# A forgetting-attention trunk on one core: the first projections taken chunk by chunk with the stream, in an order written by hand

## The chip, the core and the metric

The kernel runs on one core of a Trainium2 chip. The metric is the device time of one execution in microseconds. The engines are named as in the profile: PE (TensorE), PEld (its weight loads), DVE (VectorE), ACT (ScalarE), POOL (GpSimd) and SP (SyncE, which here only starts transfers). A *bank* below is a tile of 128 partitions by 512 float32 numbers into which PE adds up products.

## What is computed

Two layers on a stream of 512 tokens by 1024 features, float32. The first layer is forgetting attention (FoX), the second latent attention; each has an MLP with squared ReLU behind it. The change concerns the beginning of the first layer:

```python
h = rms_norm(x, norm_mix_g[0])
proj = h @ w_in                          # columns: q 1024, k 1024, v 1024, gate 16
cum = cumsum(log_sigmoid(f_logit + b_f)) # 16 heads, along the 512 tokens
s = q @ k.T / 8 + cum[query] - cum[key]  # 16 heads of 64, causal
ctx = softmax(s) @ v
x = x + ctx @ w_out
```

## The kernel before, in words

**Products.** Every float32 operand of a product is split into a high part (a cast on ACT to the format that PE multiplies fastest) and a low part (the difference, on DVE). A product is then three matmuls (`three`, L260): high by high, high by low, low by high. A matmul here is mostly 128x128 weights by 512 columns.

**Weights.** They come in pieces of up to 128x1024 (`PIECES`, L74). `fetch` (L205) starts the transfer of a piece on SP's queue into one of two buffers `raw`. `cast_piece` (L210) makes the high part `whi` on ACT, `low_piece` (L223) the low part `wlo` on DVE; each has three buffers. `piece` (L250) hands out the next piece, after it has emitted this and the one behind it.

**The stream.** It lies turned, features on partitions, in eight chunks of 128x512 (`xs[0]` to `xs[7]`). `scaled` (L282) multiplies a chunk by the norm's gain and splits it into `h[k]`. The norm's factor rstd, one number for each token, is not needed for these products and is put in when a bank is emptied.

**FoX's beginning (L471 to L559).** It is written product by product, each over all eight chunks: the gate (16 columns in a block of 128 whose rest is zero, 24 matmuls into the bank `fps`), the queries of the first two heads (24), the sums of squares over the features as matmuls with a column of ones (`token_sums`, L297) and their reciprocal root (`rsqrt_mean`, the Newton steps on POOL), the keys of the first two heads (24), rstd spread to a 128x512 tile (`rstd_tile`, L341: four matmuls and a copy), and the values of eight heads (four pieces of 24 matmuls, 96 in all, into four banks, two of the tag `sc` and two of the tag `tp`, one for each block of 128 tokens). After the first value piece the queries and keys are emptied (`qk_parts`, L494) and the forget gate is worked out (`forget_sums`, L522): a log-sigmoid on 16 partitions, then running sums along the 512 tokens in nine doubling steps of a copy and an addition each on DVE. The result goes to DRAM (`csc`) and comes back broadcast over 128 partitions (`nb`, in `start`, L576), two heads at a time. The value banks are emptied in eight halves (`value_parts`, L512).

**What sets the order.** The engines run their instructions in one fixed order each, which a scheduler works out when the program is built. Where the list `order["on"]` names an engine, its instructions are tied to the order in which they are written (L113 to L122). At FoX's beginning it names none before the change.

**The attention (L408).** The steps are one block of 128 queries of a pair of heads each, 32 in all: scores on PE, then `soft_step` (L379) on DVE and ACT, then, three steps later, the transposes of the weights on PE and the product with the values. So that PE has work while the softmax runs, `Filler` (L347) deals out other products: the queries and keys of the next pairs (`proj`), the other eight heads' values, and the beginning of the output projection. `FILL1 = (12, 18)` are the matmuls dealt out at each step and at the end of each pair. `fill.run(12)` (L643) deals out twelve ahead of the first scores.

Nearly all instructions are issued by the helper on L112 (L113 after the change), so that the profile tells them apart by their tiles and not by their lines.

Of the kernel before, what the change touches and what calls it, by code (L numbers as in the profile page):

```python
# [11 lines left out]
F32 = mybir.dt.float32  # L12
# [23 lines left out]
RP1 = 40  # L36
RP2 = 14
RSQRT_BITS = 0x5F3759DF
MASK = -1.0e30
HALF = 512  # L40
CHUNKS = 3
# [32 lines left out]
def pieces():  # L74

    out = [("f", 128)]
    out += [("qk", 1024)] * 2 + [("v", 1024)] * 4
    for p in range(1, FH // 2):
        out += [("v4", 1024)] * (2 * V4_BEFORE.count(p)) + [("qk", 1024)] * 2
    out += [("fo", 1024)] * 8  # L80
    out += [("ffn0", 1024)] * 40
    out += [("ka", 1024)] * 6
    q = [("qb_r", 384), ("qb_n", 768)]
    out += [q[0], ("kvb_n", 1024), q[1], ("kvb_v", 1024)] + q + [("kvb_n", 1024)] + q + [("kvb_v", 1024)] + q
    out += [("mo", 1024)] * 8
    out += [("ffn1", 1024)] * 32
    return out
# [10 lines left out]
def trunk(ctx: ExitStack, tc: tile.TileContext, xT, wts, gains, fing, rope, out):  # L98
# [72 lines left out]


    gsb = const.tile([P, NG], F32, name="gsb")
    nc.scalar.dma_start(gsb, gains)
# [5 lines left out]
    nc.scalar.copy(warm, ones)  # L180

    maskz = const.tile([P, S], F32, name="maskz")
    nc.gpsimd.memset(maskz, 0.0)
# [24 lines left out]
        nc.sync.dma_start(raw[:, :w], wts[OFFS[n] : OFFS[n] + P * w].rearrange("(p w) -> p w", p=P))  # L208

    def cast_piece(n):  # L210
        name, w = PIECES[n]
# [3 lines left out]
        if name == "f":  # L215
            hi = hi.rearrange("p (k c) -> p k c", c=P)[:, :, :FH]
            nc.vector.memset(f32(state["ready"][n][0]), 0.0)
            nc.vector.memset(f32(lo), 0.0)
            nc.scalar.copy(hi, fetched[n][:, :w].rearrange("p (k c) -> p k c", c=FH))
        else:  # L220
            nc.scalar.copy(hi[:, :w], fetched[n][:, :w])

    def low_piece(n):  # L223
        name, w = PIECES[n]
        hi, lo = state["ready"][n]
        src, hi, lo = fetched.pop(n)[:, :w], hi[:, :w], lo[:, :w]
        if name == "f":
            src = src.rearrange("p (k c) -> p k c", c=FH)
            hi, lo = (t.rearrange("p (k c) -> p k c", c=P)[:, :, :FH] for t in state["ready"][n])
        nc.vector.tensor_tensor(lo, src, f32(hi), op=ALU.subtract)  # L230

    def beside_piece(n):

# [2 lines left out]
    def emit_piece(n):  # L236
        if n not in fetched:
            fetch(n)
        if n in APART:

            raw = fetched.pop(n)
            his, los = [rt(), rt()], [rt(), rt()]
            for j in range(2):
                split(raw[:, j * S : (j + 1) * S], his[j], los[j])
            state["ready"][n] = [(his[k // 4][:, c], los[k // 4][:, c]) for k in range(KD) for c in [slice(k % 4 * P, k % 4 * P + P)]]
            return
        cast_piece(n)
        low_piece(n)
# [56 lines left out]
    def rstd_of(acc, dim, mult=1.0, tag="tp"):  # L305

        return rsqrt_mean(token_sums(acc, tag), dim, mult)
# [155 lines left out]

    ctxs = []
    with ExitStack() as fx:
        vpool = fx.enter_context(tc.tile_pool(name="fox_v", bufs=12))
# [3 lines left out]
        xs = [tt() for _ in range(KD)]  # L470
        for k in range(KD):  # L471
            nc.sync.dma_start(xs[k], xT[:, k, :])
            if k == 0:
                emit_piece(0)
            if k == 3:
                emit_piece(1)
# [8 lines left out]
        qk = {}  # L485
        qk_ps = []
# [22 lines left out]

        v2 = {}  # L510

        def value_parts(q, tb, src):  # L512

            vt = vpool.tile([P, 4, 2, FHD], F32R, tag="v", name=nm("v"))
# [5 lines left out]
            v2[q, tb] = vt  # L520

        def forget_sums():  # L522

            z, e = tt(), tt()
            z, e = z[:FH], e[:FH]
            nc.vector.tensor_tensor(z, fps[:FH], rstd[:FH], op=ALU.mult)
            nc.vector.tensor_scalar_add(z, z, gsb[:FH, GCOL["bf"][0] : GCOL["bf"][0] + 1])
# [5 lines left out]
            nc.vector.scalar_tensor_tensor(out=cur, in0=z, scalar=0.0, in1=e, op0=ALU.min, op1=ALU.subtract)  # L533
            nc.vector.tensor_scalar_mul(cur, cur, -1.0)
# [8 lines left out]
            return csc  # L543

        accs = [bank(t) for t in ("sc", "sc", "tp", "tp")]
        for kp in range(4):
            whi, wlo = piece("v")
            for tb in range(NB):
                for k2 in range(2):
                    k = kp * 2 + k2  # L550
                    c = slice(k2 * S, (k2 + 1) * S)
                    t = slice(tb * P, (tb + 1) * P)
                    three(accs[tb], whi[:, c], wlo[:, c], h[k][0][:, t], h[k][1][:, t], k == 0, k == KD - 1, flip=True)
            if kp == 0:
                qk[0] = [qk_parts(pp, scale) for pp, scale in zip(qk_ps, QK_SCALES)]
                csc = forget_sums()
        for tb in range(NB):
            for q in range(2):
                value_parts(q, tb, accs[tb][:, q * 256 : (q + 1) * 256])  # L559

        def v4_gen(q):
            ws = [piece("v4"), piece("v4")]
            for tb in range(NB):
                pp = bank("acc")[:, :256]
                t = slice(tb * P, (tb + 1) * P)
                for k in range(KD):
                    whi, wlo = ws[k // 4]
                    c = slice(k % 4 * 256, k % 4 * 256 + 256)
                    three(pp, whi[:, c], wlo[:, c], h[k][0][:, t], h[k][1][:, t], k == 0, k == KD - 1, flip=True)
                    if k == 3:  # L570
                        yield 6
                value_parts(q, tb, pp)
                yield 6

        nbs = {}
# [791 lines left out]
def _pack(i):  # L1367
# [1 line left out]
    parts = []  # L1369
    fw = i["fox_w_in"][0]  # L1370
    parts.append(_cols(fw, 3 * W, FH))
    parts += [_cols(fw, 0, P), _cols(fw, W, P)]
    b = _cols(fw, 2 * W, S)
    parts += [b[:, 2 * kp : 2 * kp + 2] for kp in range(4)]
    for p in range(1, 8):
# [85 lines left out]
```

## Time and profile before

| | |
|---|---|
| median of 3 runs | 1138.52 us (1138.40 to 1138.56) |
| the profiled execution | 1139.54 us, of which the span from its first to its last instruction is 1137.7 us |
| granted TensorE clock, mean | 0.995 |
| PE busy | 1117.8 us, 98% of the span |
| DVE busy | 781.3 us, 69% |
| ACT busy | 582.0 us, 51% |

Times in the profile count from the start of the span. A row of the timeline reads: start, length, engine, line, operation, output and inputs with their shapes, count, and in brackets how long the engine had been idle and what released it. A row of the chain of waits reads: start, length, engine, tile, count; it follows the work that ended last back through what released it. A row of the table by stretch has the stretch's length, then busy time and number of instructions for PE, PEld, DVE, ACT and POOL, then the granted clock, the share of the DMA engines in use and GB/s. A row of the grouped lines has the group's shape and count, busy time and mean nanoseconds of one, and the idle time before them.

Up to 52.18 us, where the first scores stand, PE was busy for 47.15 us. From there to 231 us, where the attention ends, it was busy for 177.22 us of 178.82.

### The profile page before, as it was taken

What the parts mean: (1) busy time and instruction counts of PE and PEld (TensorE: products, weight loads), DVE (VectorE), ACT (ScalarE), POOL (GpSimd) and SP (SyncE); (2) the same over time, 40 slices, a digit from 0 to 9 for tenths busy, and PEclk for the clock granted to TensorE, in tenths of its full rate; (3) what the DMA queues carried; (4) which work ended last, traced back from release to release, by engine and by line L of the source; (5) the groups of instructions that cost most, each with busy time, mean ns of one, the idle gap of its engine ahead of it and who ended that gap; (6) DMA issues with size and microseconds to landing.
All of it is one profiled execution on the core that took longest, in us unless ns stands there. A gap on an engine that the chain in (4) does not pass through costs nothing.

```text
span 1137.7 us, 14266 instructions
## 1 busy us (share of the span) xinstructions
PE 1117.8 (98%) x5340; PEld 912.9 (80%) x5340; DVE 781.3 (69%) x1420; ACT 582.0 (51%) x1060; POOL 19.5 (2%) x71
## 2 busy tenths in 40 slices
PE   8999999999999999999999999999999999999996
PEld 5777887788888888888888777788888888888885
DVE  6797888864557676577795777737265775765785
ACT  5565655644555454444364566635465545444612
POOL 1000000001000000000001100000100000000000
PEclk9999999999999999999999999999999999999998
DMA  5422222143825315212344211313442511611402
GB/s 188 131 90 96 75 74 77 54 149 93 290 80 161 99 40 186 90 57 65 102 143 137 60 46 52 111 56 97 164 166 74 184 57 56 203 56 38 130 1 75
DMA packets 36822, 116.66 MB, mean 103 GB/s; under 512 B 4224, under 2 KB 4864, under 8 KB 36752
## 3 DMA queue, kind: packets, MB, share of 16 engines
q1 hardware_dynamic: 35888, 114.15, 31.0%
q10 hardware_dynamic: 864, 1.60, 0.4%
q8 instruction: 42, 0.69, 0.3%
q14 instruction: 28, 0.23, 0.1%
HBM read 109.40 MB, written 6.32 MB: 102 GB/s over the span
## 4 chain that ended last, share of the span: by engine, by line
PE 90%; DVE 5%; ACT 2%; DMA 1%; issue 1%; SPq 0%; ACTq 0%; DVEq 0%
PE up L112 34%; PE acc L112 18%; PE go L112 17%; PE sc L112 7%; PE tp L112 7%; PE keep L112 6%; ACT t L112 2%; DVE r L112 2%; DVE t L112 2%; DVE fs L112 1%; DMA raw<-wts 1%; DVE wlo L112 1%; ACT whi L112 0%; DMA nb<-csc 0%; DVE ptl L112 0%
## 5 line engine op out<-in xcount | busy, mean ns | idle before, releaser
L112 PE MATMUL acc<-r,whi 128*128 128x512 f32 x610 | 198.7, 406 | 4.9 <-ACT whi L112 4.9
L112 PE MATMUL up<-r,r 128*128 128x512 f32 x808 | 192.7, 391 | 0.0
L112 PEld LDWEIGHTS up<-r,r 128*128 128x128 f32 x808 | 151.3, 188 | 31.4
L112 PE MATMUL up<-r,whi 128*128 128x512 f32 x544 | 171.0, 391 | 0.0
L112 DVE TENSOR_TENSOR wlo<-raw,whi 128x1024 fp32r<-128x1024 f32 (+3 forms) x95 | 111.4, 1173 | 48.7 <-ACT whi L112 47.9
L112 DVE TENSOR_TENSOR t<-s,t 128x512 fp32r<-128x512 f32 x84 | 57.9, 690 | 122.1 <-ACT t L112 122.0
L112 PEld LDWEIGHTS acc<-r,whi 128*128 128x128 f32 x610 | 112.5, 191 | 30.9 <-ACT whi L112 5.3
L112 ACT CAST whi<-raw 128x1024 fp32r<-128x1024 f32 (+3 forms) x95 | 95.4, 1008 | 71.5 <-PE acc L112 33.0
L112 ACT ACTIVATE s<-up 128x512 f32<-128x512 f32 x56 | 33.4, 597 | 190.6 <-PE up L112 190.6
L112 PE MATMUL acc<-r,wlo 128*128 128x512 f32 x305 | 121.3, 398 | 0.1
L112 PEld LDWEIGHTS up<-r,whi 128*128 128x128 f32 x544 | 101.8, 188 | 20.8
L112 PE MATMUL up<-r,wlo 128*128 128x512 f32 x288 | 112.3, 390 | 0.0
L112 PE MATMUL go<-r,t 128*128 128x512 f32 x360 | 86.5, 390 | 0.0
L112 PE MATMUL sc<-r,r 128*128 128x512 f32 (+7 forms) x480 | 82.0, 358 | 2.2 <-ACT r L112 1.0
L112 PE MATMUL go<-whi,t 128*128 128x512 f32 x240 | 78.8, 390 | 0.0
L112 PEld LDWEIGHTS go<-r,t 128*128 128x128 f32 x360 | 67.6, 188 | 14.0
L112 PEld LDWEIGHTS sc<-r,r 64*128 64x128 f32 (+1 forms) x480 | 56.1, 186 | 26.7 <-issue 9.2
L112 PEld LDWEIGHTS acc<-r,wlo 128*128 128x128 f32 x305 | 58.3, 191 | 13.2 <-DVE wlo L112 0.4
L112 PEld LDWEIGHTS up<-r,wlo 128*128 128x128 f32 x288 | 54.1, 188 | 11.3
L112 DVE TENSOR_TENSOR r<-raw,r 128x512 fp32r<-128x512 f32 x72 | 46.5, 685 | 22.2 <-ACT r L112 22.2
L112 ACT ACTIVATE s<-s 128x512 f32<-128x512 f32 x64 | 40.5, 632 | 39.6 <-DVE s L112 37.8
L112 DVE TENSOR_TENSOR r<-q,r 128x512 fp32r<-128x512 f32 x94 | 60.5, 686 | 0.0
(199 smaller groups left out, 1862.5 us busy)
## 6 DMA issues: line engine op xcount, KB each, us to landing
raw<-wts SPq DMA_DIRECT2D x122, 512.0 KB, 3.5
q<-wts SPq DMA_DIRECT2D x56, 512.0 KB, 4.6
nb<-csc SPq DMA_DIRECT2D x8, 512.0 KB, 4.7
t<-xT SPq DMA_DIRECT2D x8, 256.0 KB, 6.2
r<-xT SPq DMA_DIRECT2D x8, 256.0 KB, 5.8
xmid<-r SPq DMA_DIRECT2D x8, 256.0 KB, 7.0
r<-xmid SPq DMA_DIRECT2D x8, 256.0 KB, 4.3
xkeep<-r SPq DMA_DIRECT2D x8, 256.0 KB, 2.1
```

Source lines behind the costliest of these rows:

```text
L112: ins = fn(*args, **kw)
```

## The change

1. **Zeros.** PE begins with nine matmuls of a tile of zeros by itself, into the gate's bank, which the first real gate product overwrites (`IDLE = 9`).
2. **Gate in one block.** The gate's high and low weights stand side by side in a block 64 wide (high in columns 0 to 15, low in 32 to 47). One matmul gives high by high and low by high in separate rows of the bank, a second one high by low: two for each chunk instead of three. The two rows of results are added in `forget_sums`.
3. **Weights in four parts.** The first queries' and keys' weights are packed in four parts of 128x512, each with two chunks of the contraction of both. The stream's first chunk, the gate's weights and the second part are started from ACT's queue, the rest from SP's.
4. **Chunk by chunk.** For each chunk of the stream: scale and split it, two gate matmuls, three for queries, three for keys.
5. **Written order.** `order["on"]` names PE, DVE, ACT and SP from the beginning, and PE, DVE and ACT up to the end of the value products. Weights in there are fetched and cast by hand.
6. **Sums in the values.** The token sums and the reciprocal root, now wholly on DVE, stand behind the first six value matmuls; rstd's spreading, the emptying of queries and keys and `forget_sums` behind the thirtieth. The casts of the next pair's weights (pieces 9 and 10) are written behind that.
7. **Values by token block.** A bank is emptied whole, 512 wide, right behind its last product.
8. **Forget gate.** Signs are turned so that one multiplication less is needed, and the logarithm takes the "1 +" as its bias.
9. **Fill.** `fill.run(48)` instead of `fill.run(12)`.

```diff
+IDLE = 9
...
-    out += [("qk", 1024)] * 2 + [("v", 1024)] * 4
+    out += [("qk0", 512)] * 4 + [("v", 1024)] * 4
...
+    order["on"] = ("tensor", "vector", "scalar", "sync")
...
+        nc.scalar.dma_start(xs[0], xT[:, 0, :])
+        weights(nc.scalar, 0, fraw)
+        weights(nc.scalar, 2, raws[0][:, quarter[1]])
+        nc.scalar.copy(warm, ones)
+        nc.sync.dma_start(gsb, gains)
+        weights(nc.sync, 1, raws[0][:, quarter[0]])
+        for k in range(1, KD):
+            nc.sync.dma_start(xs[k], xT[:, k, :])
+            if k in (3, 5):
+                weights(nc.sync, (k + 3) // 2, raws[1][:, quarter[(k + 1) // 2]])
...
+        for _ in range(IDLE):
+            mm(fps, zero[:, :P], zero, start=True, stop=True)
+
+        def gate(k, j):
+            if j:
+                mm(fps[:32], fw[:, k, :32], h[k][1], start=False, stop=False)
+            else:
+                mm(fps[:64], fw[:, k], h[k][0], start=k == 0, stop=k == KD - 1)
...
-        h = [scaled(xs[k], "mix0", k) for k in range(KD)]
-        fps = bank("acc")
-        linear(fps, piece("f"), h)
+        for k in range(KD):
+            j, c = k // 2, quarter[k // 2]
+            if k % 2 == 0 and k:
+                split(raws[j // 2][:, c], his[j // 2][:, c], los[j // 2][:, c])
+            h.append(scaled(xs[k], "mix0", k))
...
+            for part in range(2):
+                gate(k, part if k < KD - 1 else 1 - part)
+            for n in range(2):
+                b = slice(c.start + (2 * n + k % 2) * P, c.start + (2 * n + k % 2 + 1) * P)
+                three(qk_ps[n], his[j // 2][:, b], los[j // 2][:, b], *h[k], k == 0, k == KD - 1)
+        order["on"] = ("tensor", "vector", "scalar")
...
-        for _ in range(2):
-            qk_ps.append(bank("acc"))
-            linear(qk_ps[-1], piece("qk"), h)
-            if len(qk_ps) == 1:
-                r = rstd_of(acc, D)
-        rstd = rstd_tile(r)
...
-            nc.vector.tensor_scalar_add(e, e, 1.0)
-            nc.scalar.activation(out=e, in_=e, func=AF.Ln)
+            nc.scalar.activation(out=e, in_=e, func=AF.Ln, bias=ones[:FH])
...
+                if (kp, tb) == (0, 0):
+                    for b in range(NB):
+                        mm(ss[:, b : b + 1], acc[:, b * P : (b + 1) * P], ones, start=True, stop=True)
+                    cast_piece(6)
+                    r = rsqrt_mean(ss, D, alone=True)
+                    low_piece(6)
+                    fetch(8)
+                elif (kp, tb) == (1, 0):
+                    rstd = rstd_tile(r)
+                    cast_piece(7)
+                    qk[0] = [qk_parts(qk_ps[0], QK_SCALES[0])]
+                    low_piece(7)
+                    qk[0].append(qk_parts(qk_ps[1], QK_SCALES[1]))
+                    cast_piece(8)
+                    low_piece(8)
+                    fetch(9)
+                    fetch(10)
+                    csc = forget_sums()
+                elif kp > 1 and tb == 0:
+                    cast_piece(kp + 7)
+                    low_piece(kp + 7)
+                    fetch(kp + 9)
+                if kp == 3:
+                    value_parts((0, 1), tb, accs[tb])
+        order["on"] = ()
...
-        fill.run(12)
+        fill.run(48)
```

Three places in the engines' orders. First DVE at the end of the forget gate's running sums, which are the rows with 16 partitions; `wlo` are low parts of weights (442 before, 431 and 461 after: the weights of the second head pair). Before:

```order
L112 COPY t_362<-t_359 16x16
L112 TENSOR_TENSOR t_362<-t_359 16x496
L112 TENSOR_TENSOR wlo_442<-raw_439,whi_441 128x1024
L112 COPY t_365<-t_362 16x32
L112 TENSOR_TENSOR t_365<-t_362 16x480
```

and after:

```order
L113 TENSOR_TENSOR t_398<-t_395 16x384
L113 COPY t_401<-t_398 16x256
L113 TENSOR_TENSOR t_401<-t_398 16x256
L113 TENSOR_TENSOR wlo_431<-raw_361,whi_430 128x1024
L113 TENSOR_TENSOR wlo_461<-raw_363,whi_460 128x1024
L113 SCALAR_TENSOR_TENSOR v_466<-sc_275,rs_294,v_466 128x8x64
L113 SCALAR_TENSOR_TENSOR v_475<-sc_276,rs_294,v_475 128x8x64
```

The low part of the second pair's first weights stood in the midst of the running sums; it now stands behind the last of them, with the other low part and the emptying of the value banks behind it.

Next PE at the end of the value products (the bank `tp_296` before, `tp_278` after) and the first fill products (banks `acc`). Before:

```order
L112 MATMUL tp_296<-wlo_412,r_157 128x512
L112 MATMUL tp_296<-whi_411,r_158 128x512
L112 MATMUL acc_493<-r_129,whi_441 128x512
L112 MATMUL acc_493<-r_130,whi_441 128x512
L112 MATMUL acc_493<-r_129,wlo_442 128x512
```

and after:

```order
L113 MATMUL tp_278<-whi_357,r_240 128x512
L113 MATMUL acc_496<-r_143,whi_430 128x512
L113 MATMUL acc_496<-r_144,whi_430 128x512
L113 MATMUL acc_527<-r_143,whi_460 128x512
L113 MATMUL acc_527<-r_144,whi_460 128x512
L113 MATMUL acc_496<-r_143,wlo_431 128x512
L113 MATMUL acc_496<-r_159,whi_430 128x512
```

The fifth fill matmul takes the low part `wlo_431` of the first place; before it was the third, with `wlo_442`.

Last PE in the last head pair: `sc` are scores, `tp` transposes of softmax weights (each 128x128), `acc` fill products of the output projection. Before:

```order
L112 MATMUL sc_2469<-r_2283,r_2176 128x256
L112 MATMUL tp_2489<-ident,t_2245 128x128
L112 MATMUL tp_2493<-ident,t_2246 128x128
L112 MATMUL acc_2301<-r_2448,whi_2297 128x512
L112 MATMUL acc_2301<-r_2449,whi_2297 128x512
L112 MATMUL acc_2301<-r_2448,wlo_2298 128x512
L112 MATMUL acc_2301<-r_2455,whi_2297 128x512
L112 MATMUL acc_2301<-r_2456,whi_2297 128x512
L112 MATMUL acc_2301<-r_2455,wlo_2298 128x512
L112 MATMUL sc_2503<-r_2283,r_2175 128x128
L112 MATMUL sc_2504<-r_2283,r_2175 128x128
```

and after:

```order
L113 MATMUL tp_2488<-ident,t_2321 128x128
L113 MATMUL sc_2467<-r_2174,r_2082 128x256
L113 MATMUL sc_2467<-r_2175,r_2082 128x256
L113 MATMUL sc_2467<-r_2174,r_2083 128x256
L113 MATMUL sc_2468<-r_2174,r_2082 128x256
L113 MATMUL sc_2468<-r_2175,r_2082 128x256
L113 MATMUL sc_2468<-r_2174,r_2083 128x256
L113 MATMUL tp_2492<-ident,t_2322 128x128
L113 MATMUL sc_2496<-r_2174,r_2082 128x128
L113 MATMUL sc_2496<-r_2175,r_2082 128x128
```

The six fill products between the last two blocks' scores are gone from there.

More of the change, by code (lines that the diff above doesn't have):

```diff
@@ L179, in trunk @@
     warm = const.tile([P, 1], F32, name="warm")
-    nc.scalar.copy(warm, ones)
     maskz = const.tile([P, S], F32, name="maskz")
@@ L214, in cast_piece @@
         state["ready"][n] = (hi, lo)
[L215 to L221, printed above, removed]
-    def low_piece(n):
[L224 to L230, printed above, removed]
+        nc.scalar.copy(hi[:, :w], fetched[n][:, :w])
+    def low_piece(n):
+        w = PIECES[n][1]
+        hi, lo = (t[:, :w] for t in state["ready"][n])
+        nc.vector.tensor_tensor(lo, fetched.pop(n)[:, :w], f32(hi), op=ALU.subtract)
     def beside_piece(n):
@@ L470, in trunk @@
         xs = [tt() for _ in range(KD)]
+        raws, his, los = (
+            [wpool.tile([P, 1024], dt, tag=t, name=nm(t), **kw) for _ in range(2)]
+            for t, dt, kw in (("raw", F32, {"bufs": 2}), ("whi", F32R, {}), ("wlo", F32R, {}))
+        )
+        zero = rt()
+        nc.vector.memset(f32(zero), 0.0)
+        fraw = f32(rt())[:, : KD * FH]
+        fw = wpool.tile([P, 1024], F32R, tag="whi", name=nm("whi"))[:, : KD * 64]
+        nc.vector.memset(f32(fw), 0.0)
+        fw = fw.rearrange("p (k c) -> p k c", c=64)
@@ new lines, in trunk, with weights @@
+        quarter = [slice(j % 2 * S, j % 2 * S + S) for j in range(4)]
+        def weights(queue, n, dst):
+            w = PIECES[n][1]
+            queue.dma_start(dst, wts[OFFS[n] : OFFS[n] + P * w].rearrange("(p w) -> p w", p=P))
+        nc.scalar.dma_start(xs[0], xT[:, 0, :])
[4 more added lines that the diff above has]
+        weights(nc.sync, 1, raws[0][:, quarter[0]])
@@ L519, in value_parts @@
             )
-            v2[q, tb] = vt
+            for j, q in enumerate(qs):
+                v2[q, tb] = vt[:, 4 * j : 4 * j + 4]
         def forget_sums():
[L524 to L527, printed above, removed]
+            u, z, e = tt(), tt()[:FH], tt()[:FH]
+            nc.vector.tensor_tensor(u[:64], fps[:64], rstd[:64], op=ALU.mult)
+            nc.scalar.copy(z, u[32 : 32 + FH])
+            nc.vector.tensor_tensor(z, z, u[:FH], op=ALU.add)
+            nc.vector.tensor_scalar(z, z, gsb[:FH, GCOL["bf"][0] : GCOL["bf"][0] + 1], -1.0, op0=ALU.add, op1=ALU.mult)
             nc.scalar.activation(out=e, in_=z, func=AF.Abs)
             nc.scalar.activation(out=e, in_=e, func=AF.Exp, scale=-1.0)
-            nc.vector.tensor_scalar_add(e, e, 1.0)
-            nc.scalar.activation(out=e, in_=e, func=AF.Ln)
+            nc.scalar.activation(out=e, in_=e, func=AF.Ln, bias=ones[:FH])
             cur = tt()[:FH]
-            nc.vector.scalar_tensor_tensor(out=cur, in0=z, scalar=0.0, in1=e, op0=ALU.min, op1=ALU.subtract)
-            nc.vector.tensor_scalar_mul(cur, cur, -1.0)
+            nc.vector.scalar_tensor_tensor(out=cur, in0=z, scalar=0.0, in1=e, op0=ALU.max, op1=ALU.add)
             d = 1
@@ L553, in trunk @@
                     three(accs[tb], whi[:, c], wlo[:, c], h[k][0][:, t], h[k][1][:, t], k == 0, k == KD - 1, flip=True)
[L554 to L559, printed above, removed]
+                if (kp, tb) == (0, 0):
[23 more added lines that the diff above has]
+        order["on"] = ()
+        order["last"].clear()
         def v4_gen(q):
@@ L1371, in _pack @@
     parts.append(_cols(fw, 3 * W, FH))
-    parts += [_cols(fw, 0, P), _cols(fw, W, P)]
+    first = [_cols(fw, 0, P), _cols(fw, W, P)]
+    parts += [np.concatenate([b[:, 2 * j : 2 * j + 2] for b in first], axis=1) for j in range(4)]
     b = _cols(fw, 2 * W, S)
```

34 lines of the change are left out of this document (22 added, 12 removed).

## The prediction

> **What bounds the kernel now.** I read the page first, then the chain of waits over the first 60 us, then the timeline of single engines there, the tables by stretch, and last who waited for whom.
>
> ```profile
> PE 1117.8 (98%) x5340; PEld 912.9 (80%) x5340; DVE 781.3 (69%) x1420; ACT 582.0 (51%) x1060; POOL 19.5 (2%) x71
> ```
>
> PE is busy for 98% of the span, so two kinds of edit count: those that take matmuls away and those that move the moments at which PE stands still. The chain over the beginning shows such a moment:
>
> ```profile
> 3.06 6.90 DMA raw<-wts
> 9.98 1.05 ACT whi L112
> 11.06 1.24 DVE wlo L112
> 12.34 8.50 PE acc L112 x36
> 20.84 0.79 PE tp L112 x8
> ...
> 26.56 1.16 PE tp L112 x8
> 27.72 2.77 PE sc L112 x12
> ...
> 49.53 2.72 PE acc L112 x12
> 52.25 0.90 PE sc L112 x6
> ```
>
> Until 12.34 the chain is a transfer of query/key weights (issued at 3.06, landed at 9.96), its cast and its low part; from there PE is never released late. Twelve matmuls take 2.72 us: 0.227 each, the price of a matmul below. The value products, 96 of them or 21.8 us, run from 27.7 to 49.5, the first scores stand at 52.25.
>
> **What the beginning costs now, and what the change makes of it.**
>
> ```profile
> 4.89 1.40 PE L112 MATMUL acc<-r,whi 128*128 128x512 f32 x2 [4.89 <-ACT whi L112]
> ...
> 6.08 0.63 PE L112 MATMUL acc<-r,wlo 128*128 128x512 f32 x1
> ...
> 13.37 0.39 PE L112 MATMUL acc<-r,wlo 128*128 128x512 f32 x1
> ```
>
> ```profile
> 1.05 0.91 DVE L112 MEMSET whi<- 128x1024 f32 x1 [0.19 <-issue]
> ```
>
> PE starts at 4.89 and its early matmuls take 0.63 us, later ones 0.39: it is cold at first. The nine products of zeros need only a memset half as wide as this one, so they can run from about 1.5 us on; at 0.39 to 0.63 each they end between 5.0 and 7.2, about when the first data is there, and cost nothing. If they don't warm PE, the few real matmuls up to 11 us run slow, as now.
>
> The gate takes 2 matmuls for each of 8 chunks instead of 3: 8 x 0.227 = 1.8 us less on PE. Gate and query/key products together are 64 matmuls, 14.5 us, now taken chunk by chunk. When can they run? The second chunk of the stream is what follows the first landing:
>
> ```profile
> 5.94 0.72 ACT L112 ACTIVATE r<-t,gsb 128x512 fp32r<-128x512 f32 x1 [1.10 <-DMA t<-xT]
> ...
> 6.70 0.75 DVE L112 SCALAR_TENSOR_TENSOR r<-t,gsb,r 128x512 fp32r<-128x512 f32 x1 [1.06 <-ACT r L112]
> ```
>
> At 5.94 0.61 MB had landed (two chunks of 0.26, gate weights, gains); at 9.96 1.66 MB: 0.26 MB/us. In the changed order the second chunk has 1.14 MB up to it (two quarters of weights of 0.26 MB go with it), so it lands at about 8.0; scaled high part 0.72 and low part 0.75 later, at 9.5, PE has all of it. The third chunk (1.40 MB) lands at 9.0, is ready at 10.5, and PE reaches it at 11.1. So from 9.5 on PE is the slower one: 7 matmuls of that chunk and 6 x 8 more, 55 x 0.227 = 12.5, and the query/key products end at E = 21.9. The values follow at once (their weights land behind the stream and are cast by 18). To their 21.8 the token sums (0.79) and the spreading of rstd (four matmuls, 0.9) now come, which stood ahead of them. Values end at E + 23.5 = 45.4, against 49.5: **4.1 us gained**, 5.9 if PE ran without a pause from 5.6 (E = 20.1), 3 if chunks come 1 us later. The token sums need the sum of squares: seven adds and one low part on DVE after the last chunk end by about 21.5, PE comes there at 23.3, so they cost no wait. The rsqrt moves from POOL to DVE, 12 small steps:
>
> ```profile
> 21.66 0.16 DVE L112 TENSOR_SCALAR rs<-tp 128x4 f32<-128x4 f32 x1 [1.31 <-PE tp L112]
> 21.86 0.38 DVE L112 TENSOR_SCALAR rs<-rs 128x4 int32<-128x4 int32 x2
> ```
>
> At 0.2 each, 2.4 us, they are over at E + 4.8, and the next low part at E + 6.0; PE wants that at E + 6.5. Covered, but with 0.5 to spare.
>
> **What the written order queues.** After the change rstd comes later relative to the values, and DVE runs its instructions as written. These rows give the pieces of the chain behind rstd:
>
> ```profile
> 27.76 0.59 ACT L112 COPY rstd<-tp 128x512 f32<-128x512 f32 x1 [0.35 <-PE tp L112]
> 29.30 1.22 ACT L112 CAST r<-t 128x512 fp32r<-128x512 f32 x2 [0.96 <-DVE t L112]
> 31.48 1.30 ACT L112 ACTIVATE t<-t 16x512 f32<-16x512 f32 x2 [0.96 <-DVE t L112]
> 33.25 1.05 ACT L112 CAST whi<-raw 128x1024 fp32r<-128x1024 f32 x1 [0.48 <-PE tp L112]
> 34.32 1.28 ACT L112 ACT_TABLE_LOAD   x1
> 35.62 0.63 ACT L112 ACTIVATE t<-t 16x512 f32<-16x512 f32 x1
> ```
>
> ```profile
> L112 DVE SCALAR_TENSOR_TENSOR t<-acc,rstd 128x512 f32<-128x512 f32 x3 | 2.0, 684 | 0.0
> L112 DVE TENSOR_TENSOR r<-t,r 128x512 fp32r<-128x512 f32 x3 | 2.0, 678 | 0.0
> ```
>
> ```profile
> 37.44 0.14 DVE L112 COPY t<-t 16x1 f32<-16x1 f32 x1
> ...
> 41.22 1.21 DVE L112 TENSOR_TENSOR wlo<-raw,whi 128x1024 fp32r<-128x1024 f32 x1
> 42.36 0.16 DVE L112 COPY t<-t 16x32 f32<-16x32 f32 x1
> ...
> 44.80 0.41 DVE L112 TENSOR_TENSOR t<-t 16x256 f32<-16x256 f32 x1
> 45.22 1.23 DVE L112 TENSOR_TENSOR wlo<-raw,whi 128x1024 fp32r<-128x1024 f32 x1
> ```
>
> The running sums of the forget gate take 37.44 to 45.21, of which 1.14 (41.22 to 42.36) was a weight's low part let in between: 6.6 alone. In the changed order, from the start of the rstd copy: copy 0.59, cast of a value weight 1.05, cast of queries 0.62, their low part 0.68, low part of a weight 1.22, keys scaled 0.68, cast 0.62, next weight's cast 1.05 (the keys' low part beside it), its low part 1.22, gate scaled 0.67, copied 0.63, added 0.67, bias 0.47, two activations 1.30, table load 1.28, logarithm 0.63, max 0.68, running sums 6.6, and only then the low part of the first weights of the next head pair, 1.22. Together 21.9; starts overlap ends by some 0.3, so 21.6.
>
> PE spreads rstd after 30 value matmuls and the sums: E + 7.6; the copy starts 1.2 later (26.56 to 27.76 now), E + 8.8. So that low part is ready at E + 30.4. PE asks for it after 96 + 4 matmuls: E + 24.4. There it waits, **6.0 us**, and the 44 further matmuls put in as cover for the scores stand behind the one that waits. DVE's own queue behind the sums holds the second low part and the emptying of the value banks, for which the scores' banks wait in turn, but those end before PE gets there. Bounds: 4 if every handover on the chain is 0.1 shorter; 7 if they are longer. Before, the same sums ended 4 us ahead of the last value product.
>
> **The clock after the wait.** A stretch with little work on PE is in the trace:
>
> ```profile
> 635.70:639.10 3.40, 2.01 (x6) 1.16 (x7) 2.13 (x4) 2.48 (x5) 0.00 (x0) 1.00 0.00 0
> 639.10:642.50 3.40, 3.40 (x9) 2.67 (x8) 3.08 (x4) 2.44 (x4) 0.00 (x0) 0.50 0.21 56
> ```
>
> After 3.40 us with PE 2.01 busy the granted clock was 0.50 for the next 3.40 us: 1.7 us of work lost. A wait of 6.0 contains such a stretch, so I add **1.7**; nothing if the slow stretch falls inside the wait, 3.1 if PE stays slow for 6.2 us, as from 4.89 to 11 or so at the start.
> The Trainium skill, "TensorE: Matmul & The Clock Gate", Part 1, states that the clock halves after one idle window of about 3.4 us and is given back after a busy one, the window running freely. By its figures, an estimate: 6.0 us hold a whole idle window in (6.0 - 3.4) / 3.4, three runs of four, which makes 1.3 in the mean. The trace agrees on the length, and its PE was not even idle.
>
> **The end of the attention.** 48 filling matmuls instead of 12 ahead of the scores are 36 fewer later; by the order they are missing in the last two head pairs.
>
> ```profile
> 52.18:82.00 29.82, 29.82 (x166) 22.55 (x166) 27.51 (x80) 19.33 (x46) 0.00 (x0) 1.00 0.29 95
> ...
> 184.75:230.88 46.13, 44.98 (x241) 33.86 (x242) 37.75 (x104) 27.43 (x71) 0.00 (x0) 1.00 0.15 47
> 202.60:222.20 19.60, 18.45 (x91) 13.24 (x90) 15.59 (x41) 10.87 (x28) 0.00 (x0) 1.00 0.18 55
> ```
>
> ```profile
> L112 DVE TENSOR_TENSOR r<-r,r 128x512 fp32r<-128x512 f32 x7 | 4.7, 687 | 0.0
> ```
>
> Columns: PE, PEld, DVE, ACT. In the stretch of the last pair (202.60 to 222.20) PE would keep 18.45 - 39 x 0.227 = 9.6 us of work, DVE 15.59 less seven splits of 0.6 that move ahead, 11.4. So DVE ends each step last there: 1.8, and scores that wait for the reduction of the step before add to it. I take **3.5**; 0 if the engines interleave as in 52.18 to 82.00, where DVE had 27.51 of 29.82 and PE didn't wait; 8 if both last pairs go at DVE's pace.
>
> **Sum.** -4.1 + 6.0 + 1.7 + 3.5 = +7.1 us. On the profiled execution's own 1139.54 (span 1137.7 and 1.84 around it) that is 1146.6; the median of the runs is 1.0 lower, 1138.52, so 1145.6. A measurement can tell about 0.2%, 2.3 us.
>
> **Rivals.**
> *The wait is hidden, faster.* If the chain from rstd to the low part took 15.6 us rather than 21.6, PE would find it ready, the clock would hold, and with a tail that costs nothing only the start counts: 1138.5 - 4.1 = 1134.4. For it: each piece is priced from rows of the old order, where handovers are mixed with other work. Against: 6.0 us is more than a quarter of the chain, and the running sums alone are 6.6 with nothing to overlap. Chance 0.15.
> *The start pays for the wait, no change.* The first loads go out on two queues; if they come so early that PE never pauses from 5.6 on, the start gains 5.9, and with clock and tail at nothing 1138.5 - 5.9 + 6.0 = 1138.6. For it: between 4.89 and 12.34 the transfers could go at more than 0.26 MB/us. Chance 0.18.
> The Trainium skill, "DMA: Bandwidth & Descriptors", section "Issuing engines are not separate DMA queues", speaks against it: transfers begun on several engines share the same 16 DMA engines, and only issue time is saved.
> *Softmax takes over from PE, slower still.* From the point where a step's fill is under DVE's time (some 12 matmuls), the last two pairs go at DVE's pace, 8, PE is thin enough there for a low clock, and the wait costs 3.1 of clock: -4.1 + 6.0 + 3.1 + 8 = 13.0, 1151.5. For it: scores stand next to scores in the new order. Against: DVE at 92% didn't hold PE up at 52 to 82. Chance 0.14.
>
> **How the numbers follow.** The forecast has 0.53. Slower by over 0.2% are the last rival and the forecast but for 0.02 at its lower end, 0.65; faster the first rival and 0.02 of the second, 0.17; within 0.2% the rest, 0.18. The range reaches from 1135.0, next to the first rival, to 1151.5, the last one; the forecast's own range is 1140 to 1151.
>
> **What would show it.** Right: value products ending near 45 us; then a wait of PE for DVE, released by wlo, of 4 to 7 us; granted clock 0.50 for about 3.4 us behind it; waits of PE for DVE in the last pairs. Wrong: no idle time of PE between the values and the first scores, or value products that end after 48.

## The result, and the profile after

| | before | after |
|---|---|---|
| median | 1138.46 us (1138.11 to 1138.56, 4 runs) | 1153.35 us (1152.35 to 1154.34, 4 runs) |
| ratio after to before | | 1.0135 (95% interval 1.0122 to 1.0147) |
| the profiled execution | 1139.54 us, span 1137.7 | 1154.34 us, span 1152.5 |
| first scores | 52.18 us | 64.30 us, with 36 more fills done |
| first MLP begins | 261.76 us | 276.75 us |

The change makes the kernel slower by 14.9 us, 1.3%. The forecast was 7.1 slower; its range ended at 1151.5, below the measured time. PE, in the page of the profile after, is as busy a share as before, which says nothing here: a PE at half clock counts as busy.

```profile
PE 1125.6 (98%) x5341; PEld 917.7 (80%) x5341; DVE 781.5 (68%) x1426; ACT 580.9 (50%) x1059; POOL 16.2 (1%) x59
```

First the beginning, in PE's timeline: the zeros, the first real products, the second chunk, and the first value product.

```profile
1.48 3.85 PE L113 MATMUL acc<-r 128*128 128x512 f32 x9 [1.48 <-DVE r L113]
5.73 1.14 PE L113 MATMUL acc<-r,whi 128*64 128x512 f32 x4 [0.39 <-DVE whi L113]
...
8.96 0.88 PE L113 MATMUL acc<-r,whi 128*32 128x512 f32 x3 [0.34 <-DVE r L113]
...
21.60 0.39 PE L113 MATMUL sc<-whi,r 128*128 128x512 f32 x1
```

The nine zeros take 3.85 us together, 0.43 each; four real products behind them take 1.14, which is full pace. Query and key products end at 21.6. Then the end of the values and the first fills, in the same timeline later on:

```profile
45.24 1.20 PE L113 MATMUL acc<-r,whi 128*128 128x512 f32 x4
52.44 0.79 PE L113 MATMUL acc<-r,wlo 128*128 128x512 f32 x1 [6.00 <-DVE wlo L113]
53.03 1.05 PE L113 MATMUL acc<-r,whi 128*128 128x512 f32 x2
...
56.47 0.62 PE L113 MATMUL acc<-r,whi 128*128 128x512 f32 x2
...
64.30 0.97 PE L113 MATMUL sc<-r,r 64*128 64x512 f32 x6
```

The values end at 45.2, 4.3 us ahead of before (49.53). Four fills later PE waits 6.00 us for the low part. Two matmuls then take 1.05 us, and 0.62 only from 56.47 on. The chain of waits shows what the low part stood behind: the last steps of the running sums.

```profile
50.85 0.41 DVE t L113
51.25 1.15 DVE wlo L113
52.40 0.04 issue
52.44 11.92 PE acc L113 x44
```

So far it went as forecast (low part ready at 52.3, wait 6.0). At 64.30 the first scores stand. Before, they and 36 more fills of 0.227 us would have stood at 52.18 + 8.17 = 60.35: the changed kernel is 3.9 us late there. When the first MLP begins it is 15.0 late. **11.0 us are lost in the attention**, where 3.5 were forecast; behind it the two kernels run alike (15.0 us late there, 14.8 at the end of the span). The waits of PE over the whole execution (columns: total, times, longest), after:

```profile
PE acc L113 <- DVE wlo L113: 6.0, 1, 6.0
PE sc L113 <- DVE sm L113: 5.3, 6, 3.4
PE acc L113 <- DVE r L113: 1.8, 2, 1.5
```

and of the second row before:

```profile
PE sc L112 <- DVE sm L112: 0.3, 1, 0.3
```

The second row is scores that wait until the softmax has read their banks. Its longest, 3.4 us, is in the last pair but one. PE there:

```profile
202.19 1.04 PE L113 MATMUL tp<-ident,t 128*128 128x128 f32 x5
206.58 1.01 PE L113 MATMUL sc<-r,r 64*128 64x256 f32 x3 [3.35 <-DVE sm L113]
```

and DVE in the same stretch:

```profile
203.62 0.69 DVE L113 TENSOR_TENSOR r<-t,r 128x512 fp32r<-128x512 f32 x1
204.23 1.22 DVE L113 TENSOR_TENSOR wlo<-raw,whi 128x1024 fp32r<-128x1024 f32 x1
205.37 0.68 DVE L113 TENSOR_TENSOR r<-raw,r 128x512 fp32r<-128x512 f32 x1
205.97 0.55 DVE L113 CUSTOM_DVE_ANT_0 t<-sc,nb 128x384 f32<-128x384 f32 x1
206.44 0.08 DVE L113 DVE_READ_ACCUMULATOR2_ANT sm<- 128x1 f32 x1
```

The softmax's reduction (CUSTOM) of 384 columns comes at 205.97, behind the low parts of the output projection's first weights (1.22 and 0.68). The fills have just run out of query and key products; the next ones need those very weights, so that nothing is left for PE. The table by stretch shows what follows the three places in which PE stands still or is thinly fed (columns: PE, PEld, DVE, ACT, POOL, then the granted clock):

```profile
45.74:49.15 3.41, 0.70 (x3) 0.26 (x2) 3.26 (x9) 2.20 (x4) 0.00 (x0) 1.00 0.00 0
49.15:55.97 6.82, 3.53 (x8) 2.81 (x9) 6.73 (x12) 0.01 (x1) 0.00 (x0) 0.50 0.37 108
202.75:206.16 3.41, 0.39 (x2) 0.14 (x1) 3.36 (x7) 3.11 (x8) 0.00 (x0) 1.00 0.01 2
206.16:212.99 6.83, 6.41 (x16) 4.63 (x17) 6.30 (x21) 3.43 (x10) 0.00 (x0) 0.50 0.49 154
233.47:236.88 3.41, 2.63 (x14) 1.94 (x14) 3.22 (x17) 2.11 (x10) 0.00 (x0) 1.00 0.00 0
236.88:240.29 3.41, 3.41 (x16) 3.22 (x15) 2.39 (x9) 2.03 (x6) 0.00 (x0) 0.50 0.00 0
```

Three times up to the first MLP the clock is granted at 0.50. Half of PE's busy time in these stretches is put down as lost work: 1.8, 3.2 and 1.7 us, an estimate.

Where the 11.0 us fall can be read by matching rows of the two timelines. Up to the last scores of the sixth pair (173.10 us before, 187.48 after) both kernels run the same 747 matmuls from their first scores on, and the changed one takes 2.3 us longer; 1.4 of it is at the second pair's scores at 85 us, which wait 0.70 and 0.17. The other 8.8 come behind. Fills in this table are matmuls into banks `acc`, and the loss is the difference in time with 0.227 us for each fill more or less:

| stretch | before: us, fills | after: us, fills | lost |
|---|---|---|---|
| seventh pair, to the first scores of the eighth | 29.50, 73 | 38.27, 79 | 7.4 |
| eighth pair, first to last scores | 19.61, 54 | 10.25, 13 | 0.0 |
| from there to the first MLP | 39.55, 90 | 40.75, 90 | 1.2 |

(One of the 36 fills falls on an edge, so that the rows add up to 8.6.) The loss is in the pair of the long wait, and behind the last pair, where the third slow stretch lies; the steps of the last pair, where the fills are missing, lose nothing against before.

### The profile page after: what moved, and what is told of

The parts are those of the page before. It is cut to its first block, busy times and chain, and to the rows that moved or that the text cites. A ratio compares the mean times of both kernels' runs of the same rounds, so it can differ in the third digit from the quotient of the medians.

```text
span 1152.5 us, 14278 instructions
## 1 busy us (share of the span) xinstructions
PE 1125.6 (98%) x5341; PEld 917.7 (80%) x5341; DVE 781.5 (68%) x1426; ACT 580.9 (50%) x1059; POOL 16.2 (1%) x59
## 4 chain that ended last, share of the span: by engine, by line
PE 88%; DVE 7%; ACT 3%; DMA 1%; issue 1%; ACTq 0%; SPq 0%; DVEq 0%
PE up L113 34%; PE acc L113 18%; PE go L113 17%; PE sc L113 6%; PE tp L113 6%; PE keep L113 6%; DVE t L113 3%; ACT t L113 2%; DVE r L113 2%; DVE wlo L113 1%; DVE fs L113 1%; DMA t<-xT 0%; ACT whi L113 0%; ACT r L113 0%; DMA nb<-csc 0%
## 5 line engine op out<-in xcount | busy, mean ns | idle before, releaser
L113 PE MATMUL acc<-r,whi 128*128 128x512 f32 (+1 forms) x610 | 197.9, 406 | 1.1 <-ACT r L113 0.4
L113 PEld LDWEIGHTS acc<-r,whi 128*128 128x128 f32 (+1 forms) x610 | 112.2, 191 | 28.3 <-issue 1.9
L113 PE MATMUL acc<-r,wlo 128*128 128x512 f32 x297 | 117.9, 398 | 6.0 <-DVE wlo L113 6.0
L113 PE MATMUL sc<-r,r 128*128 128x512 f32 (+7 forms) x480 | 85.6, 360 | 6.6 <-DVE sm L113 5.3
```

What stands on the lines that cost most here:

```text
L113: ins = fn(*args, **kw)
```

## The experiments

Two theories stood at the outset. *Sum of a wait and a tail*: the late gate sums cost a wait at the beginning, and the 36 fills used up early cost the tail. Its rival, *one late softmax*: everything follows from the softmax starting later, and taking the wait away only moves it. The first reduction on DVE, before:

```profile
54.31 0.68 DVE L112 CUSTOM_DVE_ANT_0 t<-sc,nb 128x512 f32<-128x512 f32 x1
```

and after, 12.7 us later:

```profile
67.04 0.68 DVE L113 CUSTOM_DVE_ANT_0 t<-sc,nb 128x512 f32<-128x512 f32 x1
```

**e1, the kernel before with 48 fills.**

```diff
-        fill.run(12)
+        fill.run(48)
```

> The kernel before with one edit: 48 filling matmuls ahead of the first scores instead of 12. Its last head pairs have PE's rows in the changed kernel's order, its beginning is the old one. If the tail's cost comes from the 36 fills that are used up early, the tail loses what it lost in the changed kernel (9.9 us more than before from 200 us on), and the beginning nothing: 1138.5 + 9.9 = 1148.4, within 1.5. Rival: the tail's cost comes from the late start of the softmax and the new order of the beginning; then this kernel stays at 1138.5, within 1.

Measured: 1148.07 us (1146.66 to 1149.33), ratio 1.0088 (1.0073 to 1.0103). The fills alone cost 10.5 us against the kernel before on the same chip (1137.56), with the old beginning. The wait is the same one, in PE's timeline:

```profile
202.25 1.00 PE L112 MATMUL sc<-r,r 64*128 64x256 f32 x3 [3.35 <-DVE sm L112]
```

**e2, the changed kernel with 12 fills.**

```diff
-        fill.run(48)
+        fill.run(12)
```

> The changed kernel with 12 fills ahead of the first scores instead of 48. If the fills used up early are the tail's cost, 9.9 us come back there, and at the beginning the softmax, whose gate sums land at 61.5 us, holds up the second or third scores by 1 to 3 us more: 1153.4 - 9.9 + 2 = 1145.5, from 1144 to 1147. Rival, the late softmax makes the tail's cost: 1152 to 1156.

Measured: 1148.16 us (1146.87 to 1149.88), ratio 1.0090 (1.0075 to 1.0105): 5.2 us come back, not 8. The tail is that of before again, but the beginning pays more than I had put down: with fewer fills the second scores wait for the softmax, and the clock is granted at 0.50 once more behind that.

```profile
60.39 0.39 PE L113 MATMUL acc<-r,wlo 128*128 128x512 f32 x1
62.14 0.44 PE L113 MATMUL sc<-r,r 64*128 64x384 f32 x1 [1.36 <-DVE sm L113]
```

```profile
64.00:67.41 3.41, 3.41 (x9) 2.31 (x7) 3.41 (x9) 2.52 (x6) 0.00 (x0) 0.50 0.00 0
```

**e3, the low parts let in between the running sums, 48 fills.** The casts and low parts of pieces 9 and 10 move into the loop of `forget_sums`; those of piece 11 are now written by hand too, behind the value banks' emptying.

```diff
                 cur, d = nxt, 2 * d
+                if d in (4, 32):
+                    cast_piece(9 + d // 32)
+                    low_piece(9 + d // 32)
...
                 elif kp > 1 and tb == 0:
-                    cast_piece(kp + 7)
-                    low_piece(kp + 7)
                     fetch(kp + 9)
...
+        cast_piece(11)
+        low_piece(11)
         order["on"] = ()
```

> The changed kernel with the low parts of the second pair's two weights let in between the running sums, so that PE finds them at 46 us, 48 fills as in the change. If the wait for the low part is a cost by itself, 6.2 us of it and 1.7 of slow clock go: 1145.5, within 1. Rival: the gate sums, 2.3 us later for it and back from memory at 63 us, hold the softmax, whose second step PE then waits for at about 60: 4 to 7 us of the gain are lost again, 1149 to 1153.

Measured: 1145.90 us (1145.36 to 1148.02), ratio 1.0073 (1.0056 to 1.0091). The rival falls: the wait was a cost by itself, and the 48 fills do cover the later gate sums. What is left of the wait:

```profile
47.08 0.50 PE L113 MATMUL acc<-r,wlo 128*128 128x512 f32 x1 [1.31 <-DVE wlo L113]
```

**e4, the changed kernel without the zeros** (`IDLE = 0`).

> The changed kernel without the nine products of zeros. If they warm PE, the first eight real matmuls from 5.7 us take 0.43 instead of 0.23 and PE may stay slow until 9 to 11 us: 0.2 to 1.2 us more than 1153.4. If PE waits for the second chunk anyway and is fast by then: no difference, within 0.3.

Measured: 1155.15 us (1152.49 to 1155.59), ratio 1.0146 (1.0130 to 1.0162). That is above both expectations, but the interval overlaps with the changed kernel's, so that the time alone settles nothing. The timeline does, for the beginning: PE's first products go at about half pace until 9.3 or so, and the first fills stand at 45.88 instead of 45.24, 0.6 us later.

```profile
5.80 1.97 PE L113 MATMUL acc<-r,whi 128*64 128x512 f32 x4 [5.80 <-DVE whi L113]
7.57 0.63 PE L113 MATMUL acc<-r,wlo 128*128 128x512 f32 x1
```

**e5, e6, e7, e10, e11, e12: the gate first, with 12, 18, 24, 6, 36 and 48 fills.** If the late chain from rstd to the gate sums is what spoils the earlier start, it should be moved up. rstd is spread after 18 value matmuls, and the gate goes ahead of the queries' and keys' emptying; what fills its gaps is taken from them.

```diff
+                elif (kp, tb) == (0, 2):
+                    rstd = rstd_tile(r)
+                elif (kp, tb) == (0, 3):
+                    csc = forget_sums()
+                elif (kp, tb) == (1, 3):
+                    cast_piece(9)
+                    low_piece(9)
+                    fetch(11)
+                    qk[0] = []
+                    for t, hi in zip(qts, qhs):
+                        lo = rt()
+                        nc.vector.tensor_tensor(lo, t, f32(hi), op=ALU.subtract)
+                        qk[0].append((hi, lo))
+                elif (kp, tb) == (2, 3):
+                    cast_piece(10)
+                    low_piece(10)
+                    fetch(12)
```

Inside `forget_sums`, the scaling of queries and keys stands ahead of the logarithm, their casts and piece 8's behind it, and piece 8's low part behind the second doubling step; piece 7 is cast and split with piece 6, and piece 11 behind the values, as in e3.

> The changed kernel with the forget gate taken ahead of the queries' and keys' emptying: rstd spread after 18 value matmuls instead of 30, the gate's steps and running sums right behind it on DVE and ACT, the next weights' low parts behind or between them; 12 fills. If the late chain from rstd to the gate sums and the early fills are the whole loss, the sums end near 44 instead of 51 and are back from memory at 51 to 53 instead of 61.5; PE finds the low part at 46 and waits 2 to 3 us for the second scores; the tail is that of before: 1138.0 - 4.1 + 3 = 1137, from 1135 to 1138.5. If something else of the written beginning costs (value banks emptied whole, other buffers), 1140 or more.

> As the one before, with 18 fills: the softmax's start is covered by 1.4 us more work, the tail has 6 fills less. If the tail's loss grows evenly with the fills (9.5 us for 36), 1.6 more there and 1.4 less at the beginning: as with 12, within 1. If the tail's loss comes in one piece, when the output projection's first weights fall on a step without fills, it can be 1.4 less: 1135.5.

> As the two before, with 24 fills. Evenly growing loss in the tail: 3.2 more there, 2 to 3 less at the beginning, 1137 to 1138. Loss in one piece: 1134.5 if the piece does not fall, 1142 if it does.

> The gate-first kernel with 6 fills. Its first scores stand 1.4 us earlier, at 46.6; the gate sums land at 48.8 as before, so that the second scores wait up to 1 us, and the tail has 6 fills more: 1134.5 to 1136.5, no difference to 12 fills within 1.

> The gate-first kernel with 36 fills. From 200 us on the kernels with 12, 18 and 24 fills lost 4 to 5 us of PE's time and those with 48 13.5 to 14. If the loss sets in with the steps of the last two pairs that have no fill between scores (with 24 there is one, with 36 three to four, with 48 five to six), it is 7 to 10 here: 1138.0 - 4.1 + 1.5 at the beginning + 4 = 1139.5, from 1138 to 1141. If it sets in only with 48: 1136.5 to 1138.

> The gate-first kernel with 48 fills: the beginning without its wait, the tail of the changed kernel. If tail and beginning add up: 1138.0 - 4.1 + 1.5 + 9.9 = 1145.3, within 1.5; the rival, that the tail's loss needs the late beginning of the change too: 1138 or less.

Measured, with the two moments that separate beginning and attention. "Early" is how far ahead of the kernel before the first scores stand, for the same work (52.18 us and 0.227 for each fill over 12); "lost" is what is lost between there and the first MLP, against before; "late" is the part of it that comes behind the last scores of the sixth pair, up to which all these kernels run the same work from their first scores on (745 to 749 recorded matmuls). The times of the moments are those of one profiled execution each. The medians come from several chips, on which the kernel before had medians of 1137.6 to 1138.5.

| kernel | fills | median us | ratio (interval) | first scores | MLP begins | early | lost | late |
|---|---|---|---|---|---|---|---|---|
| e10 | 6 | 1136.86 | 0.9988 (0.9978 to 0.9997) | 47.00 | 260.30 | 3.8 | 2.4 | 0.5 |
| e5 | 12 | 1135.17 | 0.9976 (0.9966 to 0.9985) | 47.93 | 258.65 | 4.3 | 1.1 | 0.9 |
| e6 | 18 | 1136.92 | 0.9988 (0.9978 to 0.9997) | 49.23 | 260.24 | 4.3 | 2.8 | 0.3 |
| e7 | 24 | 1137.47 | 0.9994 (0.9984 to 1.0003) | 51.01 | 261.11 | 3.9 | 3.2 | 0.2 |
| e11 | 36 | 1144.83 | 1.0054 (1.0039 to 1.0069) | 53.47 | 269.13 | 4.2 | 11.5 | 9.3 |
| e12 | 48 | 1146.21 | 1.0067 (1.0050 to 1.0084) | 56.29 | 269.13 | 4.1 | 11.4 | 9.4 |
| e3 | 48 | 1145.90 | 1.0073 (1.0056 to 1.0091) | 57.74 | 269.97 | 2.6 | 10.8 | 8.6 |
| e1 | 48 | 1148.07 | 1.0088 (1.0073 to 1.0103) | 60.52 | 272.16 | -0.2 | 10.2 | 8.5 |
| e4 | 48 | 1155.15 | 1.0146 (1.0130 to 1.0162) | 65.27 | 276.24 | -4.9 | 9.6 | 7.8 |
| after | 48 | 1153.35 | 1.0135 (1.0122 to 1.0147) | 64.30 | 276.75 | -3.9 | 11.0 | 8.8 |
| e2 | 12 | 1148.16 | 1.0090 (1.0075 to 1.0105) | 56.63 | 270.29 | -4.5 | 4.1 | -0.1 |

Three things follow. The earlier start is real, and it is kept when the gate goes first: e5 is faster than before. There the low part stands ready as the values end, and the first reduction comes at 50.59 us. DVE:

```profile
42.45 0.41 DVE L113 TENSOR_TENSOR t<-t 16x256 f32<-16x256 f32 x1
42.79 1.21 DVE L113 TENSOR_TENSOR wlo<-raw,whi 128x1024 fp32r<-128x1024 f32 x1
...
50.59 0.69 DVE L113 CUSTOM_DVE_ANT_0 t<-sc,nb 128x512 f32<-128x512 f32 x1 [0.15 <-DVE nb L113]
```

and PE, which runs on from the values through the fills to the first two scores:

```profile
45.12 0.62 PE L113 MATMUL acc<-r,whi 128*128 128x512 f32 x2
45.57 0.39 PE L113 MATMUL acc<-r,wlo 128*128 128x512 f32 x1
...
47.93 0.97 PE L113 MATMUL sc<-r,r 64*128 64x512 f32 x6
```

Second, beginning and tail add up: e1, e3, e4, e12 and the changed kernel have five different beginnings and lose 7.8 to 9.4 late. Third, the loss is not so much for each fill. From 6 to 24 fills the late part stays between 0.2 and 0.9, at 36 it is all there: e11 missed its expectation (1138 to 1141). Two more expectations missed by little: e6 was to be within 1 us of e5 and is 1.8 above it, e10 is 1.7 above it. The time of e7 is the one expected of an evenly growing loss, but for another reason: 3.0 of its 3.2 us are lost ahead of the last two pairs, 2.0 of them in waits of scores for the softmax at 56 and 73 us. With 24 fills the low parts of the output projection's weights fall beside a softmax step of 128 columns, and PE waits 0.15 and 0.26 us; with 36 beside one of 256 columns, and it waits 2.15; with 48 beside one of 384, and it waits 3.35. DVE of e7:

```profile
198.33 1.22 DVE L113 TENSOR_TENSOR wlo<-raw,whi 128x1024 fp32r<-128x1024 f32 x1
199.47 0.69 DVE L113 TENSOR_TENSOR r<-t,r 128x512 fp32r<-128x512 f32 x1
200.07 0.29 DVE L113 CUSTOM_DVE_ANT_0 t<-sc,nb 128x128 f32<-128x128 f32 x1
```

**e8, the output projection's weights taken up one by one, in the changed kernel; e9, the same in e5.** In `out_begin`, which deals out the beginning of the output projection:

```diff
-        mine = [(bank(t), blocks(piece(name))) for t in tags]
-        outs += mine
+        mine = []
         for ks in ((0, 2), (2, 4), (4, 6), (6, 7)):
-            for pp, w in mine:
+            for n, t in enumerate(tags):
+                if ks[0] == 0:
+                    mine.append((bank(t), blocks(piece(name))))
+                    outs.append(mine[n])
+                pp, w = mine[n]
                 for k in range(*ks):
                     while ready() <= k:
                         yield 1000
                     three(pp, *w[k], *part(k), k == 0, False)
                 yield 3 * (ks[1] - ks[0])
```

> The changed kernel, with 48 fills, in which the filling part of the output projection takes up its three weight pieces one by one, each with its first products, and not all three ahead of the first product. All before it stays as it was; at 204 us the low parts of these weights (1.2 and twice 0.7 on DVE) stand behind the softmax's reductions, not ahead of them. If these low parts make the long wait of the tail, it falls from 3.4 to 1.5 us, products come between the scores, and the slow clock behind it (6.8 us at half) goes or is halved: 1153.4 - 1.9 - 1.7 to 3.4 = 1148 to 1150. Rival: it is the missing fills alone, DVE ends every step last: 1152 to 1154.

> The gate-first kernel with 12 fills and the output projection's weight pieces taken up one by one. There PE waits 1.1 us at that place and the clock holds: 0 to 1 us less than the gate-first kernel's 1135.2.

Measured: e8 1150.81 us (1148.92 to 1151.66), ratio 1.0102 (1.0084 to 1.0121), 2.5 less than the changed kernel, where 3.4 to 5.4 were expected. The reduction comes right behind the split at 204.22, as meant (DVE):

```profile
204.22 0.69 DVE L113 TENSOR_TENSOR r<-t,r 128x512 fp32r<-128x512 f32 x1
204.83 0.55 DVE L113 CUSTOM_DVE_ANT_0 t<-sc,nb 128x384 f32<-128x384 f32 x1
```

PE waits 1.2 us there, the clock holds, and of the 7.4 us lost in the seventh pair 2.9 are left (33.74 us with 79 fills). Over the whole attention 3.2 of the 11.0 are won (first scores 64.69, MLP 273.89). For the last pair, with 13 fills left, still waits, and now the slow clock comes there, for twice as long as in the changed kernel:

```profile
227.70:231.11 3.41, 3.04 (x18) 2.08 (x16) 3.12 (x12) 2.68 (x10) 0.00 (x0) 1.00 0.00 0
231.11:237.94 6.83, 6.41 (x25) 5.95 (x25) 4.31 (x18) 2.95 (x9) 0.00 (x0) 0.50 0.00 0
```

e9: 1133.89 us (1132.72 to 1134.90), ratio 0.9957 (0.9942 to 0.9973), 4.1 us under the kernel before of the same chip (1138.03) and 1.3 under e5, where 0 to 1 was expected. Its first scores stand at 48.14 and its MLP begins at 257.40: nothing of the early start is lost in the attention. It beats both kernels.

## Why the prediction was wrong

*The beginning: right.* Query and key products ended at 21.6 (forecast 21.9), values 4.3 us earlier (4.1). The second chunk was on PE at 8.96 (9.5). The sums of squares and the reciprocal root on DVE cost no wait.

*The zeros: right.* They end at 5.3, within the forecast 5.0 to 7.2, and cost nothing. The first real products run at full pace behind them and at about half pace without them; e4 puts 0.6 us on that, which the sum didn't name.

*The wait for the low part: right.* 6.0 us by the trace, 6.0 forecast: the chain from the copy of rstd (30.44) to the low part (52.40) took 22.0 us, 21.6 in the forecast. e3 shows that it was a cost by itself. The rival that it is hidden is out, and so is the rival that the start pays for the wait.

*The clock behind the wait: right in size, in part by luck.* 1.8 us (49.15 to 55.97, half of 3.53 busy), 1.7 forecast. The slow stretch was not one of 3.4 us behind the wait but one of 6.8, and half of it fell inside the wait, where it cost nothing. The same price had to be put down behind the waits of the tail too, where it came to 4.9 us; the forecast stopped at the first.

*The end of the attention: the step that failed.* It was put as: "DVE ends each step last there: 1.8, and scores that wait for the reduction of the step before add to it. I take **3.5**", with 8 as upper end. Measured: 11.0. The stretch that it was read from, the last pair's steps, lost nothing: it took 10.25 us for 19.61 with 41 fills fewer, and DVE was busy for 9.28 us of it, PE for 9.47, where the forecast had 11.4 and 9.6. The two overlapped; PE waited for DVE there for 0.8 us in all. What the forecast had at nothing was the pair before, with 7.4 us; another 1.2 come behind the last pair, and 2.3 ahead of both (1.4 of them at the second pair's scores). I had averaged DVE's work over a pair and compared it with PE's. The runs showed one place instead: when the fills change from query and key products to the output projection, weights' low parts stand ahead of a reduction on DVE just as PE has no products that don't need those weights. The wait of 3.4 us and the slow clock behind it, 3.2, are 6.6 of the 7.4. e8 takes the low parts away from there, and 2.9 are left of the 7.4; e7 and e11 show that the loss comes in one piece between 24 and 36 fills. The last rival had the tail's size about right (8) and named the low clock there, but DVE's pace was not the mechanism.

*What stays open.* How much of the loss is the clock's can't be said for sure: no run held the clock fixed. In e1 and e12 one slow stretch of 10.24 us stands behind the long wait and none at the last pair, in the changed kernel one of 6.83 and one of 3.41, in e8 only one of 6.83 at the last pair, where PE's waits were as short as in the changed kernel (0.37 and 0.42 us, 0.36 and 0.41 there). e8 does two things at once: the low parts leave the reduction's way, and PE's next products need one weight piece and not three; no run separates them. Of the 2.9 us that e8 still loses in the seventh pair, waits of 1.2, 0.2 and 0.5 us are a part, and the rest stays open. Nor was it tried whether e3 or e12 with spread weights would keep 48 fills cheap.

## What to carry to other kernels

An early start brings its full gain only when the longest chain behind it moves too: put the step that others wait for (here the gate's sums) ahead of its neighbours before adding cover. Cover is not free, since each product dealt out early is missing later. Look for the place where one kind of cover ends and the next begins, and see what stands ahead of the waited-for step in the queue there. Put a price on the clock behind every wait, not only the first.

## What the runs showed of the hardware

The granted clock fell to 0.50 for 3.41, 6.83 or 10.24 us, one, two or three times the same window, and stayed there although PE was busy for most of the slow time. The three slow stretches of the changed kernel begin 46 and 9 such windows apart (49.15, 206.16, 236.88). It did not take an idle window: ahead of 236.88 in the changed kernel PE was busy for 2.63 of 3.41 us, and in e12 for 1.99 of 3.41 ahead of a slow stretch of 10.24, in which it was busy for 8.23. In e8 (above) it was even 3.04 of 3.41. Yet from 83.28 to 86.69 in the changed kernel, ten such windows behind 49.15, PE was busy for only 2.54 of 3.41 and the clock stayed at 1.00. So the profile's busy time is not what the clock goes by; what it does go by no run here shows. The stretch of e12:

```profile
192.97:196.38 3.41, 1.99 (x13) 1.03 (x11) 3.29 (x9) 3.41 (x9) 0.00 (x0) 1.00 0.00 0
196.38:206.62 10.24, 8.23 (x20) 6.06 (x21) 7.90 (x23) 4.72 (x14) 0.00 (x0) 0.50 0.34 103
```

The Trainium skill, "TensorE: Matmul & The Clock Gate", Part 1, gives a free-running window of about 3.4 us, half clock after an idle one and full clock after a busy one. The length agrees, and so does the even spacing; but no idle window was needed for half clock, and a busy one didn't always bring full clock back: in e11 the clock stayed at 0.50 from 225.31 to 232.14, two windows in which PE was busy throughout.

At the start the granted clock doesn't show the slow pace. In e4 the first eight products take 3.48 us, 0.44 each, while the granted clock reads 1.00 from 5.80 to 9.50; later ones take 0.227.
